# Low parts of sixteen query-weight tiles and four expert tiles split in the feed-forward on VectorE and kept in DRAM, and compressed inputs split in halves

## The chip, the cores and the metric

The kernel runs on one core of a Trainium2 chip. The metric is the device time of one execution in microseconds. TensorE (PE in the profile) does the matmuls; VectorE (DVE), ScalarE (ACT) and GpSimd (POOL) do the element-wise work; SyncE (SP) issues the loads of weights. fp32 products are made of three matmuls of a reduced type (fp32r): each operand is split into a high part and the low part that is left over.

## The reference, cut to what matters

Two blocks of a network on 512 tokens of width 1024. In the first the feed-forward matters here, in the second the compressed keys and values of the attention and the queries of a layer with 16384 experts (PEER).

```python
def hybrid_layer(x, p_i, ...):
    ...
    h = rmsnorm(x, g_ffn)
    g, u = jnp.split(h @ w_gate_up, 2, axis=-1)
    x = x + (jax.nn.silu(g) * u) @ w_down
    ...

def nsa_mixer(q, k_cmp, v_cmp, ...):
    ...
    def compress(t, w1, w2):
        blk = t[:, cmp_idx] + cmp_pos[:, None, :]
        blk = blk.transpose(0, 1, 3, 2, 4).reshape(B, n_cmp, G, CMP_LEN * dk)
        return jax.nn.gelu(blk @ w1) @ w2

    kc = compress(k_cmp, cmp_k_w1, cmp_k_w2)
    vc = compress(v_cmp, cmp_v_w1, cmp_v_w2)
    ...

def peer_ffn(x, w_q, sub_keys, expert_u, expert_v):
    q = _rms((xt @ w_q).reshape(T, P_HEADS, P_KEY_DIM)).astype(x.dtype)
    s1 = jnp.einsum('thd,hnd->thn', q[..., :half], sub_keys[:, 0])
    s2 = jnp.einsum('thd,hnd->thn', q[..., half:], sub_keys[:, 1])
    v1, i1 = lax.top_k(s1, P_TOPK)
    v2, i2 = lax.top_k(s2, P_TOPK)
    ...
    def chunk(args):
        xc, ec, gc = args
        a = jnp.einsum('cd,ckd->ck', xc, expert_u[ec])
        w = (gc * jax.nn.gelu(a)).astype(x.dtype)
        return jnp.einsum('ck,ckd->cd', w, expert_v[ec])
    ...
```

## The kernel before, in words

Activations lie transposed, 128 features by 512 tokens to a tile. A weight tile is 128x1024 fp32 (512 KB). `weights` (L50) brings one in: `load` (L45) issues a DMA on SP's queue into one of three `wraw` buffers, and `split` (L57) makes the high part `whi` by a cast on ACT (L58) and the low part `wlo` by a subtract (L59), on DVE, or on POOL where the caller says so. `whi` and `wlo` have two buffers each. `mm3` (L66) is one product: weights high by x high (L71), weights high by x low (L72), weights low by x high (L73). `linear` (L79) does a whole tile: 8 times `mm3`, 24 matmuls into one PSUM bank.

Each engine has a program in a fixed order, written by a scheduler; SP issues all loads of weights from one program, in order, and a DMA whose buffer is not free holds up those behind it.

The first block ends with `ffn` and `ple`. `ffn` goes over 44 w_gu tiles in pairs (gate and up); a pair's products on DVE are L229 and L231 to L233, and the low part `fl` of the result (L59 by way of `split`). Then come 8 rounds of three w_down pieces.

In the second block `compress` (L919) is called twice, for keys (kv=0) and values (kv=1). It splits its input `blk` into `bs` (L943; one buffer for both calls), on DVE for the keys and on POOL for the values, and multiplies by four weight tiles: for each of 16 positions a matmul with the high part (L949) and one with the low part (L950).

`queries` (L1414) takes the 8 heads of the PEER layer in turn. Each has two weight tiles (halves), the first's low part made on DVE, the second's on POOL:

```python
w = [s.weights(I["peer_w_q"][2 * h + half], D, G if half else V) for half in range(2)]
```

Between heads it makes the hidden values of expert chunks (`hidden`, `hidden_chunk`, L1655 and L1671; one weight tile `peer_ut` each), the first ones from a list AWAY whose results are stored to `spill`: none for heads 0 to 2, one for head 3, two for each later head, and 11 behind the last. On DVE stand, beside the low parts, the choice of the 16 best keys (`choose_steps`, L1563) and the norm of x (L1549), whose product xn is split into xsh (ACT) and xsl (DVE, L64).

Of the kernel before, what the change touches and what calls it, by code (L numbers as in the profile page):

```python
# [11 lines left out]
F32 = mybir.dt.float32  # L12
# [6 lines left out]
KF = 22  # L19
WARM = 9  # L20
# [5 lines left out]
class K:  # L26
    def __init__(s, tc, I, O, ctx):
        s.tc, s.nc, s.I, s.O = tc, tc.nc, I, O
        s.cst = ctx.enter_context(tc.tile_pool(name="cst", bufs=1))
        s.res = ctx.enter_context(tc.tile_pool(name="res", bufs=2))  # L30
        s.wp = ctx.enter_context(tc.tile_pool(name="wp", bufs=2))
        s.psum_stack = ctx.enter_context(ExitStack())
        s.n = 0
        s.banks(8)
# [15 lines left out]
    def weights(s, src, n, eng=None):  # L50
        raw = s.load(src, n)
        hi = s.wp.tile([128, 1024], F32R, tag="whi", name=s.name("whi"))
        lo = s.wp.tile([128, 1024], F32R, tag="wlo", name=s.name("wlo"))
        s.split(raw[:, :n], hi[:, :n], lo[:, :n], eng)
        return hi, lo

# [22 lines left out]
    def linear(s, src, a, nk=KD, eng=None, bank=()):  # L79
# [3 lines left out]
        for k in range(nk):  # L83
            s.mm3(ps, w, a, k, k, k == 0, k == nk - 1)
        return ps
# [59 lines left out]
    def block1(s):  # L145
# [50 lines left out]
        with ExitStack() as c1:  # L196
# [13 lines left out]
            x1 = s.ffn(act, xh, xl, sq, x1)  # L210
            x1 = s.ple(act, xh, xl, x1)
        return x1

    def ffn(s, act, xh, xl, sq, x):
# [3 lines left out]
        with tc.tile_pool(name="fa", bufs=1) as fa, tc.tile_pool(name="fk", bufs=2) as fk:  # L218
# [17 lines left out]
            for c in range(KD):  # L236
                ps = s.psum()
                for k0, k1 in ((0, 8), (8, 15), (15, 22)):
                    w = s.weights(I["w_down"][c][:, k0 * 128:k1 * 128], (k1 - k0) * 128)
                    for k in range(k0, k1):  # L240
                        s.mm3(ps, w, (fh, fl), k - k0, k, k == 0, k == KF - 1)
                TT(x1[:, c, :], ps, x[:, c, :], op=ALU.add)
# [260 lines left out]
class K2(K):  # L503
# [415 lines left out]
    def compress(s, ap, kv, ps, r):  # L919
# [22 lines left out]
        bs = ap.tile([128, 16, 2, 64], F32R, tag="bs", name=s.name("bs"))  # L942
        s.split(blk, bs[:, :, 0, :], bs[:, :, 1, :], s.nc.gpsimd if kv else None)  # L943
        ph = s.turns(*TB_)
        for q in range(4):
            wh, wl = (x.rearrange("p (a b) -> p a b", a=4) for x in s.weights(I[("cmp_k_w1", "cmp_v_w1")[kv]][q], 1024, CWE and s.nc.gpsimd))
            for i in range(4):
                j = q * 4 + i
                mm(ph[:, 0:256], bs[:, j].rearrange("p a b -> p (a b)"), wh[:, i, :], start=j == 0, stop=False, skip_group_check=True)  # L949
                mm(ph[:64, 0:256], bs[:, j, 0, :], wl[:, i, :], start=False, stop=j == 15, skip_group_check=True)  # L950
# [432 lines left out]
class K3(K2):  # L1383
    def experts(s, hT):
# [29 lines left out]
    def queries(s, ctx, eT):  # L1414
# [58 lines left out]
        for h in range(8):  # L1473
            qT = qk.tile([128, 2, T], F32, tag="qT", name=s.name("pqT"))
            ss = []
            w = [s.weights(I["peer_w_q"][2 * h + half], D, G if half else V) for half in range(2)]
# [194 lines left out]
    def hidden_chunk(s, c, eng):  # L1671
        w = s.weights(s.I["peer_ut"][c], D, eng)
        ps = s.pp.tile([128, 512], F32, tag="po", name=s.name("psA"), bufs=2)
        for k in range(KD):
            s.mm3(ps[:, :TD], w, (s.xh[:, :, 128:], s.xl[:, :, 128:]), k, k, k == 0, k == KD - 1)
# [190 lines left out]
LAG = 32  # L1866
# [52 lines left out]
```

## Time and profile before

| | before |
|---|---|
| median of 3 runs | 2421.92 us (2421.37 to 2426.93) |
| the profiled execution, its own time | 2424.03 us |
| its span in the profile | 2422.3 us |
| PE busy | 2365.4 us, 98% |
| DVE busy | 1779.3 us, 73% |
| ACT busy | 1018.3 us, 42% |
| POOL busy | 688.1 us, 28% |
| granted TensorE clock, mean over the span | 0.991 |
| read from and written to DRAM | 401.71 MB, 30.41 MB |

The span is the time from the first to the last instruction that the profiler saw. Busy time is a share of the whole span, so an engine may be idle in one stage and full in another. A wait in the profile is put down to the instruction that ended last of those waited for. A granted clock of 1 is 2.4 GHz.

### The profile page before, as it was taken

To read this page: it belongs to the slowest core of one execution; us is meant where nothing else is said; L and a number is where in the kernel's file an instruction comes from. 1 tells how busy PE (TensorE), PEld (TensorE's weight loads), DVE (VectorE), ACT (ScalarE), POOL (GpSimd) and SP (SyncE) were. 2 spreads that over 40 slices of the span, in tenths; PEclk is the share of its full clock that TensorE was granted. 3 is DMA by queue.
4 is the path that set the end of the run, shared out by engine and by line. 5 is a ranking of instruction groups with operands and counts; after the bars stand their busy time and mean duration, and the time that the engine had idled before them with its cause. 6 is when DMAs were issued, how large, how long until landed. Compare 5 with 4: busy or idle time off the path is not lost.

```text
span 2422.3 us, 34482 instructions
## 1 busy us (share of the span) xinstructions
PE 2365.4 (98%) x12831; PEld 2027.7 (84%) x12831; DVE 1779.3 (73%) x3426; ACT 1018.3 (42%) x1634; POOL 688.1 (28%) x693
## 2 busy tenths in 40 slices
PE   8999999999999999999799999999899999999999
PEld 7888888888888777677688999998798889989887
DVE  7777664555435658776899898796788878889797
ACT  5444343222224466763344555433333333333333
POOL 1000001000011204334455000255555555555441
PEclk9999999999999999999899999999999999999999
DMA  4232322222333331002133555648999999999895
GB/s 134 96 105 90 102 96 96 96 96 96 97 96 108 106 105 44 1 1 84 59 119 128 179 218 207 226 160 290 333 332 348 350 341 326 351 347 360 302 342 203
DMA packets 166072, 434.37 MB, mean 179 GB/s; under 512 B 15120, under 2 KB 71312, under 8 KB 164368
## 3 DMA queue, kind: packets, MB, share of 16 engines
q1 hardware_dynamic: 126736, 294.80, 36.1%
q0 software_dynamic: 36864, 134.23, 14.8%
q10 hardware_dynamic: 2304, 3.15, 0.3%
q8 instruction: 100, 1.64, 0.3%
q14 instruction: 68, 0.56, 0.1%
HBM read 401.71 MB, written 30.41 MB: 178 GB/s over the span
## 4 chain that ended last, share of the span: by engine, by line
PE 44%; DVE 5%; DMA 2%; ACT 1%; issue 1%; POOL 0%; ACTq 0%; DVEq 0%; POOLq 0%
PE ps L1792 7%; PE ps L1793 7%; PE psA L73 7%; PE psA L71 7%; PE ps L1791 7%; PE psA L72 6%; PE ps L1733 3%; DMA wraw<-peer_ut 1%; DVE wlo L59 1%; DMA wraw<-peer_v 1%; PE ps L73 0%; PE ps L71 0%; DVE ix L1583 0%; PE ps L72 0%; DVE ix L1580 0%
## 5 line engine op out<-in xcount | busy, mean ns | idle before, releaser
L58 ACT CAST whi<-wraw 128x1024 fp32r<-128x1024 f32 (+3 forms) x322 | 330.3, 1026 | 708.9 <-issue 250.1
L59 DVE TENSOR_TENSOR wlo<-wraw,whi 128x1024 fp32r<-128x1024 f32 (+2 forms) x314 | 387.6, 1235 | 205.4 <-ACT whi L58 197.3
L71 PE MATMUL psA<-xsh,whi 128*128 128x384 f32 x1024 | 346.6, 339 | 3.6 <-ACT whi L58 3.3
L73 PE MATMUL psA<-xsh,wlo 128*128 128x384 f32 x1024 | 345.3, 337 | 4.0 <-DVE wlo L59 4.0
L72 PE MATMUL psA<-xsl,whi 128*128 128x384 f32 x1024 | 343.5, 335 | 0.0
L72 PE MATMUL ps<-xl,whi 128*128 128x512 f32 x864 | 337.3, 390 | 4.3 <-DVE xl L64 4.3
L73 PE MATMUL ps<-xh,wlo 128*128 128x512 f32 x864 | 337.8, 391 | 0.5 <-DVE wlo L59 0.5
L71 PE MATMUL ps<-xh,whi 128*128 128x512 f32 x864 | 336.8, 391 | 0.7 <-ACT whi L58 0.5
L1792 PE MATMUL ps<-vl,wh 128*128 128x512 f32 x768 | 299.9, 390 | 3.9 <-DVE vl L59 3.9
L1793 PE MATMUL ps<-vh,wl 128*128 128x512 f32 x768 | 298.1, 389 | 0.0
L1791 PE MATMUL ps<-vh,wh 128*128 128x512 f32 x768 | 243.8, 390 | 4.5 <-ACT vh L58 4.5
L304 POOL TENSOR_TENSOR sq<-sq,sqt 128x512 f32<-128x512 f32 x18 | 28.8, 1601 | 711.9 <-ACT sqt L303 708.3
L71 PEld LDWEIGHTS psA<-xsh,whi 128*128 128x128 f32 x1024 | 192.4, 188 | 10.6 <-ACT whi L58 4.5
L73 PEld LDWEIGHTS psA<-xsh,wlo 128*128 128x128 f32 x1024 | 192.2, 188 | 8.2 <-DVE wlo L59 5.6
L72 PEld LDWEIGHTS ps<-xl,whi 128*128 128x128 f32 x864 | 162.5, 188 | 39.5 <-DVE xl L64 5.5
L72 PEld LDWEIGHTS psA<-xsl,whi 128*128 128x128 f32 x1024 | 192.4, 188 | 2.9
L73 PEld LDWEIGHTS ps<-xh,wlo 128*128 128x128 f32 x864 | 162.4, 188 | 36.9 <-DVE wlo L59 3.2
L71 PEld LDWEIGHTS ps<-xh,whi 128*128 128x128 f32 x864 | 162.5, 188 | 35.2 <-ACT whi L58 1.0
L58 ACT CAST wh<-w 128x384 fp32r<-128x384 f32 x128 | 65.7, 513 | 255.0 <-issue 150.5
L1792 PEld LDWEIGHTS ps<-vl,wh 128*128 128x128 f32 x768 | 144.1, 188 | 32.2 <-DVE vl L59 5.2
L1791 PEld LDWEIGHTS ps<-vh,wh 128*128 128x128 f32 x768 | 143.7, 188 | 32.0 <-ACT vh L58 5.7
L1793 PEld LDWEIGHTS ps<-vh,wl 128*128 128x128 f32 x768 | 144.2, 188 | 28.3
(549 smaller groups left out, 4676.9 us busy)
## 6 DMA issues: line engine op xcount, KB each, us to landing
wraw<-peer_ut SPq DMA_DIRECT2D x128, 512.0 KB, 5.2
wraw<-peer_v SPq DMA_DIRECT2D x128, 512.0 KB, 6.2
wraw<-w_in SPq DMA_DIRECT2D x58, 512.0 KB, 3.3
gdram<-blk SPq DMA_DIRECT2D x12, 2048.0 KB, 7.2
wraw<-w_gu SPq DMA_DIRECT2D x44, 512.0 KB, 3.2
gt<-gdram SPq DMA_DIRECT2D x32, 704.0 KB, 8.1
wraw<-w_out SPq DMA_DIRECT2D x16, 512.0 KB, 3.3
wraw<-peer_w_q SPq DMA_DIRECT2D x16, 512.0 KB, 3.3
```

Of the source, the lines that this page charges most:

```text
L58: s.nc.scalar.copy(hi, raw)
L59: (eng or s.nc.vector).tensor_tensor(lo, raw, hi.bitcast(F32), op=ALU.subtract)
L71: mm(ps, wh, ah[:, ka, :], start=start, stop=False)
L72: mm(ps, wh, al[:, ka, :], start=False, stop=False)
L73: mm(ps, wl, ah[:, ka, :], start=False, stop=stop)
L304: nc.gpsimd.tensor_tensor(sq[:, 0, :], sq[:, 0, :], t, op=ALU.add)
L1733: last = mm(ps[:, i * 128:i * 128 + 128], os[:, j * 4 + i], f[:, j * 4 + i], start=f is f0, stop=f is f2)
L1791: mm(Y[tt][b], wh[:, sl], vh[:, vs], start=False, stop=False, skip_group_check=True)
L1792: mm(Y[tt][b], wh[:, sl], vl[:, vs], start=False, stop=False, skip_group_check=True)
L1793: mm(Y[tt][b], wl[:, sl], vh[:, vs], start=False, stop=last, skip_group_check=True)
```

## The change

A generator, `ahead`, makes the low parts of 20 weight tiles early: the 16 tiles of peer_w_q and the first four chunks of AWAY. Each tile is taken in four quarters of 128x256. For each of the 80 pieces SP loads 128 KB into one of three buffers `alo`, DVE casts it to the one buffer `ahi`, DVE subtracts that from `alo` in place, and SP stores the result in a DRAM tile `lows`. `linear` and the w_down loop of `ffn` call `tick`, which emits pieces; in the scheduler's order they stand three to a w_gu tile, from the fifth tile on, and none in w_down. Later `weights` takes such a tile's low part by a DMA of 512 KB from `lows` into `wlo`; the high part is still a cast on ACT. For the four U chunks the matmuls stand in another order: all 16 with the high weights first, then the 8 with the low ones. In `compress` the block is cast and subtracted in two halves, each with two buffers, always on DVE.

```diff
+SHARE = 1.0
+EARLY = 20
+LOWS = 3
-    def weights(s, src, n, eng=None):
+    def weights(s, src, n, eng=None, low=None):
         raw = s.load(src, n)
         hi = s.wp.tile([128, 1024], F32R, tag="whi", name=s.name("whi"))
         lo = s.wp.tile([128, 1024], F32R, tag="wlo", name=s.name("wlo"))
-        s.split(raw[:, :n], hi[:, :n], lo[:, :n], eng)
+        if low is None:
+            s.split(raw[:, :n], hi[:, :n], lo[:, :n], eng)
+        else:
+            s.nc.scalar.copy(hi[:, :n], raw[:, :n])
+            s.nc.sync.dma_start(lo[:, :n].bitcast(F32), low)
         return hi, lo
...
+    def ahead(s, todo):
+        nc = s.nc
+        d = s.dram.tile([len(todo), 128, D], F32, name="lows")
+        pieces = [(i, slice(q * 256, q * 256 + 256)) for i in range(len(todo)) for q in range(4)]
+        made = []
+
+        def ask():
+            if len(made) < len(pieces):
+                i, sl = pieces[len(made)]
+                lo = s.home.tile([128, 256], F32R, tag="alo", name=s.name("alo"), bufs=LOWS)
+                nc.sync.dma_start(lo.bitcast(F32), todo[i][1][:, sl])
+                made.append(lo)
+
+        def store(n):
+            i, sl = pieces[n]
+            nc.sync.dma_start(d[i][:, sl], made[n].bitcast(F32))
+            if sl.stop == D:
+                s.low[todo[i][0]] = d[i]
+        ask()
+        for n in range(len(pieces)):
+            ask()
+            if n:
+                store(n - 1)
+            lo = made[n]
+            hi = s.home.tile([128, 256], F32R, tag="ahi", name=s.name("ahi"), bufs=1)
+            nc.vector.tensor_copy(hi, lo.bitcast(F32))
+            nc.vector.tensor_tensor(lo, lo.bitcast(F32), hi.bitcast(F32), op=ALU.subtract)
+            yield
+        store(len(pieces) - 1)
+        yield
...
+    def tick(s, share):
+        if s.early is not None:
+            s.due += share
+            while s.due >= 1:
+                s.due -= 1
+                next(s.early, None)
...
@@ -82,6 +133,7 @@
         ps = s.psum(*bank)
         for k in range(nk):
             s.mm3(ps, w, a, k, k, k == 0, k == nk - 1)
+        s.tick(SHARE)
...
-            x1 = s.ffn(act, xh, xl, sq, x1)
-            x1 = s.ple(act, xh, xl, x1)
+            with tc.tile_pool(name="early", bufs=1) as s.home:
+                s.early = s.ahead(s.later())
+                x1 = s.ffn(act, xh, xl, sq, x1)
+                x1 = s.ple(act, xh, xl, x1)
+                for _ in s.early:
+                    pass
+                s.early = None
...
@@ -239,6 +296,7 @@
                     w = s.weights(I["w_down"][c][:, k0 * 128:k1 * 128], (k1 - k0) * 128)
                     for k in range(k0, k1):
                         s.mm3(ps, w, (fh, fl), k - k0, k, k == 0, k == KF - 1)
+                    s.tick(SHARE * (k1 - k0) / 8)
...
-        bs = ap.tile([128, 16, 2, 64], F32R, tag="bs", name=s.name("bs"))
-        s.split(blk, bs[:, :, 0, :], bs[:, :, 1, :], s.nc.gpsimd if kv else None)
+        bs = [ap.tile([128, 8, 2, 64], F32R, tag="bs", name=s.name("bs"), bufs=2) for _ in range(2)]
+        for hf in range(2):
+            s.split(blk[:, hf * 8:hf * 8 + 8], bs[hf][:, :, 0, :], bs[hf][:, :, 1, :])
         ph = s.turns(*TB_)
         for q in range(4):
             wh, wl = (x.rearrange("p (a b) -> p a b", a=4) for x in s.weights(I[("cmp_k_w1", "cmp_v_w1")[kv]][q], 1024, CWE and s.nc.gpsimd))
             for i in range(4):
                 j = q * 4 + i
-                mm(ph[:, 0:256], bs[:, j].rearrange("p a b -> p (a b)"), wh[:, i, :], start=j == 0, stop=False, skip_group_check=True)
-                mm(ph[:64, 0:256], bs[:, j, 0, :], wl[:, i, :], start=False, stop=j == 15, skip_group_check=True)
+                mm(ph[:, 0:256], bs[j // 8][:, j % 8].rearrange("p a b -> p (a b)"), wh[:, i, :], start=j == 0, stop=False, skip_group_check=True)
+                mm(ph[:64, 0:256], bs[j // 8][:, j % 8, 0, :], wl[:, i, :], start=False, stop=j == 15, skip_group_check=True)
...
+    def later(s):
+
+        u = list(AWAY) + list(range(LAG))
+        todo = [(("q", i), s.I["peer_w_q"][i]) for i in range(16)] + [(("u", c), s.I["peer_ut"][c]) for c in u]
+        return todo[:EARLY]
...
-            w = [s.weights(I["peer_w_q"][2 * h + half], D, G if half else V) for half in range(2)]
+            w = [s.weights(I["peer_w_q"][2 * h + half], D, G if half else V, s.low.get(("q", 2 * h + half))) for half in range(2)]
...
     def hidden_chunk(s, c, eng):
-        w = s.weights(s.I["peer_ut"][c], D, eng)
+        low = s.low.get(("u", c))
+        w = s.weights(s.I["peer_ut"][c], D, eng, low)
         ps = s.pp.tile([128, 512], F32, tag="po", name=s.name("psA"), bufs=2)
-        for k in range(KD):
-            s.mm3(ps[:, :TD], w, (s.xh[:, :, 128:], s.xl[:, :, 128:]), k, k, k == 0, k == KD - 1)
+        x = s.xh[:, :, 128:], s.xl[:, :, 128:]
+        if low is None:
+            for k in range(KD):
+                s.mm3(ps[:, :TD], w, x, k, k, k == 0, k == KD - 1)
+        else:
+            for i, j in ((0, 0), (0, 1), (1, 0)):
+                for k in range(KD):
+                    s.nc.tensor.matmul(ps[:, :TD], w[i][:, k * 128:k * 128 + 128], x[j][:, k, :], start=i + j + k == 0, stop=i == 1 and k == KD - 1)
```

On SP in the feed-forward there were only the loads of w_gu, one to a tile (`wraw` are the load buffers). Before:

```order
L47 DMA wraw_428_2992<-w_gu 128x1024
L47 DMA wraw_432_3023<-w_gu 128x1024
L47 DMA wraw_438_3063<-w_gu 128x1024
L47 DMA wraw_442_3094<-w_gu 128x1024
L47 DMA wraw_448_3134<-w_gu 128x1024
```

In the changed kernel, `alo` being the buffers of the pieces and `lows` the DRAM tile (L80 loads a piece, L85 stores one, L54 loads a weight tile):

```order
L54 DMA wraw_481_3297<-w_gu 128x1024
L85 DMA lows_2938<-alo_513_3494 128x256
L85 DMA lows_2938<-alo_521_3540 128x256
L80 DMA alo_535_3623<-peer_w_q 128x256
L85 DMA lows_2938<-alo_527_3577 128x256
L80 DMA alo_541_3660<-peer_w_q 128x256
L80 DMA alo_549_3706<-peer_w_q 128x256
L54 DMA wraw_489_3343<-w_gu 128x1024
L85 DMA lows_2938<-alo_535_3623 128x256
L85 DMA lows_2938<-alo_541_3660 128x256
L85 DMA lows_2938<-alo_549_3706 128x256
L80 DMA alo_555_3743<-peer_w_q 128x256
```

Each w_gu load is now followed by three stores and three loads of pieces; a load of a piece stands behind the store that frees its buffer.

On DVE in the same place, one pair of w_gu tiles, before (`fg` is the product of gate and up, `fl` its low part):

```order
L229 TENSOR_TENSOR fg_436_3054<-ps_431_2998,r_425_2981 128x512
L59 TENSOR_TENSOR fl_2901<-fg_426_2983,fh_2900 128x512
L59 TENSOR_TENSOR wlo_440_3066<-wraw_438_3063,whi_439_3065 128x1024
L231 TENSOR_TENSOR fg_436_3054<-fg_436_3054,ft_437_3055 128x512
L232 TENSOR_TENSOR fg_436_3054<-fg_436_3054,r_425_2981 128x512
L233 TENSOR_TENSOR fg_436_3054<-ps_435_3029,fg_436_3054 128x512
L59 TENSOR_TENSOR wlo_444_3097<-wraw_442_3094,whi_443_3096 128x1024
L59 TENSOR_TENSOR fl_2901<-fg_436_3054,fh_2900 128x512
```

And in the changed kernel (L95 the cast of a piece, L96 its subtract; L286 and L288 to L290 are the products that were L229 and L231 to L233):

```order
L286 TENSOR_TENSOR fg_473_3251<-ps_464_3183,r_430_3000 128x512
L110 TENSOR_TENSOR wlo_477_3263<-wraw_475_3260,whi_476_3262 128x1024
L288 TENSOR_TENSOR fg_473_3251<-fg_473_3251,ft_474_3252 128x512
L95 CAST ahi_564_3792<-alo_555_3743 128x256
L289 TENSOR_TENSOR fg_473_3251<-fg_473_3251,r_430_3000 128x512
L96 TENSOR_TENSOR alo_555_3743<-alo_555_3743,ahi_564_3792 128x256
L95 CAST ahi_570_3829<-alo_563_3789 128x256
L96 TENSOR_TENSOR alo_563_3789<-alo_563_3789,ahi_570_3829 128x256
L95 CAST ahi_578_3875<-alo_569_3826 128x256
L96 TENSOR_TENSOR alo_569_3826<-alo_569_3826,ahi_578_3875 128x256
L290 TENSOR_TENSOR fg_473_3251<-ps_470_3220,fg_473_3251 128x512
L110 TENSOR_TENSOR wlo_483_3300<-wraw_481_3297,whi_482_3299 128x1024
```

The split of a weight tile (L110) now stands behind the casts and subtracts of three pieces.

On SP in the queries, heads 3 to 4, the loads of peer_w_q, keys and peer_ut stood alone. Before:

```order
L47 DMA wraw_1535_9883<-peer_ut 128x1024
L47 DMA wraw_1541_9918<-peer_w_q 128x1024
L47 DMA wraw_1544_9924<-peer_w_q 128x1024
L1429 DMA keys_1586_10214<-keys 128x256
L47 DMA wraw_1568_10107<-peer_ut 128x1024
L47 DMA wraw_1573_10141<-peer_ut 128x1024
L1429 DMA keys_1621_10459<-keys 128x256
L47 DMA wraw_1579_10176<-peer_w_q 128x1024
L47 DMA wraw_1582_10182<-peer_w_q 128x1024
```

In the changed kernel (L65 loads a low part, with the buffer `wlo` of the tile):

```order
L65 DMA wlo_1675_10203<-lows_2938 128x1024
L65 DMA wlo_1678_10209<-lows_2938 128x1024
L54 DMA wraw_1703_10411<-peer_w_q 128x1024
L54 DMA wraw_1706_10417<-peer_w_q 128x1024
L65 DMA wlo_1699_10379<-lows_2938 128x1024
L54 DMA wraw_1730_10600<-peer_ut 128x1024
L1495 DMA keys_1748_10707<-keys 128x256
L65 DMA wlo_1705_10414<-lows_2938 128x1024
L54 DMA wraw_1735_10634<-peer_ut 128x1024
L54 DMA wraw_1741_10669<-peer_w_q 128x1024
L65 DMA wlo_1708_10420<-lows_2938 128x1024
```

The low parts stand between the loads of whole tiles, each about two tiles behind its own `wraw` load.

## Rows read from the trace of the kernel before

**Rows 1.** The page: busy time of each engine, share of the span, instructions.
```profile
PE 2365.4 (98%) x12831; PEld 2027.7 (84%) x12831; DVE 1779.3 (73%) x3426; ACT 1018.3 (42%) x1634; POOL 688.1 (28%) x693
```

**Rows 2.** Windows view, feed-forward: length; PE, PEld, DVE, ACT, POOL busy; PEclk; DMA share; GB/s.
```profile
476.00:636.00 160.00, 160.00 (x707) 132.48 (x707) 83.11 (x102) 45.73 (x58) 0.00 (x0) 1.00 0.30 98
```

**Rows 3.** Timeline, PE, feed-forward: first matmuls of two w_gu tiles (start, length, us).
```profile
559.92 0.39 PE L71 MATMUL ps<-xh,whi 128*128 128x512 f32 x1
...
565.36 0.39 PE L71 MATMUL ps<-xh,whi 128*128 128x512 f32 x1
```

**Rows 4.** Timeline, DVE, the same stretch: one pair of w_gu tiles.
```profile
560.12 0.69 DVE L229 TENSOR_TENSOR fg<-ps,r 128x512 f32<-128x512 f32 x1 [2.71 <-PE ps L73]
561.02 1.22 DVE L59 TENSOR_TENSOR wlo<-wraw,whi 128x1024 fp32r<-128x1024 f32 x1 [0.21 <-ACT whi L58]
...
571.00 0.69 DVE L229 TENSOR_TENSOR fg<-ps,r 128x512 f32<-128x512 f32 x1 [2.71 <-PE ps L73]
```

**Rows 5.** One tile's instructions: lwl, 128x256 subtracts on DVE (ns, min/median/max).
```profile
L59 DVE TENSOR_TENSOR lwl<-wraw,lwh x8: 411/416/2022, 752.5 to 798.3; 128x256 fp32r<-128x256 f32 x8
```

**Rows 6.** One tile's loads: w_ple, 128 KB each, on SP's queue.
```profile
DMA to landing us min/median/max: 1.9/2.0/3.7
```

**Rows 7.** The stores to spill, 192 KB each, 1200 to 1345 us.
```profile
DMA to landing us min/median/max: 1.8/2.6/5.4
```

**Rows 8.** The three stores to spill of 1296 to 1312 us alone.
```profile
DMA to landing us min/median/max: 1.8/1.8/1.8
```

**Rows 9.** Waits of PE, 835 to 900 us (us in total, times, longest).
```profile
PE ps L949 <- POOL bs L59: 4.9, 1, 4.9
```

**Rows 10.** Timeline, POOL and PE, second compress.
```profile
854.48 2.34 POOL L59 TENSOR_TENSOR bs<-blk,bs 128x1024 fp32r<-128x1024 f32 x1 [9.85 <-ACT bs L58]
...
857.25 0.41 PE L950 MATMUL ps<-wlo,bs 128*64 128x256 f32 x1
...
857.46 0.41 PE L949 MATMUL ps<-whi,bs 128*128 128x256 f32 x1
...
863.52 0.28 PE L949 MATMUL ps<-whi,bs 128*128 128x256 f32 x1
...
863.63 0.28 PE L950 MATMUL ps<-wlo,bs 128*64 128x256 f32 x1
```

**Rows 11.** Waits of PE, 1140 to 1200 us.
```profile
PE ps L71 <- ACT xsh L63: 8.4, 2, 6.1
PE ps L73 <- DVE wlo L59: 4.3, 1, 4.3
PE ps L72 <- DVE xsl L64: 1.4, 1, 1.4
```

**Rows 12.** Waits of PE, 1200 to 1260 us.
```profile
PE psA L73 <- DVE wlo L59: 1.0, 2, 0.6
```

**Rows 13.** Waits of PE, 1260 to 1335 us.
```profile
PE psA L73 <- DVE wlo L59: 2.9, 2, 1.6
```

**Rows 14.** Timeline, DVE and POOL, PEER queries.
```profile
1159.78 0.60 DVE L64 SCALAR_TENSOR_TENSOR xsl<-xn,c_vec,xsh 128x384 fp32r<-128x384 f32 x1
...
1164.07 2.36 POOL L59 TENSOR_TENSOR wlo<-wraw,whi 128x1024 fp32r<-128x1024 f32 x1 [10.15 <-ACT whi L58]
...
1164.35 2.50 DVE L64 SCALAR_TENSOR_TENSOR xsl<-xn,c_vec,xsh 128x384 fp32r<-128x384 f32 x1
```

**Rows 15.** Timeline, PE, PEER queries, heads 2 and 3.
```profile
1186.35 0.39 PE L73 MATMUL ps<-xsh,wlo 128*128 128x512 f32 x1
...
1192.74 0.79 PE L73 MATMUL ps<-xsh,wlo 128*128 128x512 f32 x1 [4.31 <-DVE wlo L59]
1193.34 0.63 PE L71 MATMUL ps<-xsh,whi 128*128 128x512 f32 x1
1193.76 0.63 PE L72 MATMUL ps<-xsl,whi 128*128 128x512 f32 x1
```

**Rows 16.** DMA issues, 1140 to 1340 us (KB each, median us to landing).
```profile
wraw<-peer_w_q SPq DMA_DIRECT2D x12, 512.0 KB, 3.4
```

More of the change, by code (lines that the diff above doesn't have):

```diff
@@ L31, in __init__ @@
         s.wp = ctx.enter_context(tc.tile_pool(name="wp", bufs=2))
+        s.dram = ctx.enter_context(tc.tile_pool(name="dr", bufs=1, space=bass.MemoryType.DRAM))
         s.psum_stack = ctx.enter_context(ExitStack())
         s.n = 0
+        s.low = {}
+        s.early = None
+        s.due = 0.0
         s.banks(8)
@@ L209, in block1 @@
                     s.add_and_norm(I["w_out"], (mh, ml), xT, x1, "g_ffn", xh, xl, sq, wk)
-            x1 = s.ffn(act, xh, xl, sq, x1)
-            x1 = s.ple(act, xh, xl, x1)
+            with tc.tile_pool(name="early", bufs=1) as s.home:
[4 more added lines that the diff above has]
+                    pass
+                s.early = None
         return x1
```

## The prediction

> **What bounds the kernel now.** I read the page first: TensorE (PE) is busy 98% of the span, VectorE (DVE) 73%, GpSimd (POOL) 28% [rows 1]. So only the few idle stretches of PE, and those where its clock is low, can be won, and any new wait of PE is lost at once. The windows view shows the stretch into which the change puts work: in the feed-forward PE is busy for 160 of 160 us at a granted clock of 1.00 (of 2.4 GHz), DVE for 83 us, POOL for none [rows 2]. The timeline gives the pace there: the first matmuls of two w_gu tiles start 5.44 us apart [rows 3], and DVE's program repeats after two tiles, 10.88 us [rows 4]. The view of PE's waits shows what can be won: 4.9 us in the second `compress`, behind a subtract on POOL [rows 9], and in the PEER queries 4.3, 1.4, 1.0 and 2.9 us behind low parts of weights or of x [rows 11 to 13]. The 8.4 us for xsh in rows 11 come from the chain of the norm (columns, square root, rows, product), which the change leaves as it is.
>
> **A. The pieces in the feed-forward.** 80 pieces, each a load of 128 KB, a cast and a subtract of 128x256 on DVE, and a store of 128 KB. By the order there are three to a w_gu tile, so they fill some 27 tiles, 147 us.
>
> *DVE.* The subtract is 0.416 us [rows 5]. A DVE cast of this form is not in the trace; I bound it by 0.416 above (the same elements, one operand fewer) and by nothing below, and take 0.416, its nearest row. Three pieces to a tile are 6 x 0.83 = 5.0 us a pair, on top of 83.11/160 x 10.88 = 5.65 [rows 2]: 10.6 of 10.88 us. That fits, hidden under PE, with 0.2 us to spare. The Trainium skill ("VectorE: DVE Perf Modes", section "Mode 2×_2P — use both read ports for one tensor") lets a one-source copy in SBUF run at two elements a cycle, where a two-source subtract cannot: the cast would then be about 0.28 us (an estimate: from 0.416 for 256 elements and 1.22 for 1024, half the part that grows with them) and the pair 9.8 us. The cost is nothing by either; by the rule the margin is wider.
>
> *The buffers.* There are three `alo` buffers and SP issues in order: the load of piece n+3 stands behind the store of piece n and waits for its landing. One turn of a buffer is load 2.0 [rows 6], one product of the feed-forward that DVE may be in 0.69 [rows 4], cast 0.42, subtract 0.42, store 1.8, the three spill stores that had the queue to themselves, each larger than a piece [rows 8]: 5.3 us, against 5.44 for the tile that uses all three. What pieces delay is the split of the next w_gu tile: `wlo` is behind casts that wait for loads. Now it is done at 562.24 [rows 4], while the tile starts at 565.36 [rows 3] and needs it two matmuls later, at 565.8: 3.5 us of slack, once. So 26 turns of L us cost 26 x (L - 5.44) - 3.5: nothing up to L = 5.57. I take nothing (5.3 us). The upper end has the slowest w_ple load, 3.7 [rows 6]: L = 7.0, +37 us. The w_gu load ahead of each round on the same queue is what could make it so.
>
> **B. compress.** The second `compress` casts and subtracts its whole block only when the first has left the single `bs` buffer, and the subtract takes 2.34 us on POOL [rows 10], for which PE stands 4.9 us [rows 9]. Behind the gap 17 matmuls run at half clock, 1.2 GHz: 0.21 us apart where the later ones are 0.11 [rows 10], 1.6 us. With two half buffers the first half of the second block can be made while PE is in the second half of the first, and a half on DVE is 0.6 us (half of the 1.22 in rows 4). What is late next is the weights' own split: DVE needs 1.22 us for a tile that PE eats in 8 x 0.11 = 0.9; a first tile or two will wait for it. I take -4; ends 0 (the block itself is late) and -6.5 (gap and half clock both gone).
>
> **C. PEER queries.** Low parts arrive by DMA. Off go 8 subtracts on POOL, 8 on DVE, and 4 for U chunks.
> - xsl 0.60 us alone, 2.50 beside POOL's `wlo` subtract [rows 14]: -1.9, since PE waits for xsl, and the choice of keys and the norm stand behind it on DVE.
> - the gap of 4.3 us before head 3 [rows 11]: the low part lands 3.4 us [rows 16] after its buffer is free, at about 1186.4 with the last matmul of head 2 that reads it [rows 15], so at 1189.8 to 1190.8 (SP has other loads ahead), where PE stands for it from 1188.4 (1192.74 less the 4.3) [rows 15]: 1.4 to 2.4 us stay. -2.4.
> - 9 matmuls at half clock behind the gap, 0.42 apart [rows 15] where the pace is 0.227 [rows 3]: -1.8, since a gap half as long is nearer to those after which the clock stayed.
> - the 1.0 and half of the 2.9 us for `wlo` in rows 12 and 13 (the other half belongs to chunks that are split as before): -2.4.
> - what is late next: the low part of a first half waits for the two-buffer `wlo` ring behind a U chunk, two or three times 0.5 us: +1.2.
>
> Together -7.3. Ends: +3 (nothing gained, and such waits three times) and -12 (all of rows 12 and 13 and the 4.3 as well).
>
> **The sum.** 0 - 4 - 7.3 = -11.3, against the profiled execution of 2424.03 us, so 2413. That execution is 2.1 over the median of the three runs, 2421.92; against the median 2411. The 180 added DMAs (160 of 128 KB, 20 of 512 KB) all stand on SP's queue; their price is the one in A and C.
>
> **Rivals.**
> 1. *The piece loop is longer than a tile* (slower). Store, load, cast, subtract, store is one circle through SP's queue, and w_gu's load is in it. It decides from L = 5.57; the whole is slower than before by over 0.3% from L = 6.3 (26 x 0.86 - 3.5 = 19, less 11). If in two rounds of three a transfer meets the w_gu load and takes 3.7 instead of 2.0 [rows 6], L = 6.4: +22, 2433. For it: DMA runs beside PE at 0.30 of its engines' time already [rows 2], DVE has but 0.2 us to spare in a pair, and the slowest spill store took 5.4 [rows 7]. Against it: most of the small transfers are at 2.0 and below.
> 2. *Stores like the median one*, 2.6 us [rows 7]: L = 2.0 + 0.69 + 0.83 + 2.6 = 6.1, +14: 2425, no difference to be measured. The spill stores ran beside more traffic than the feed-forward has, which speaks against it. The Trainium skill ("DMA: Bandwidth & Descriptors", section "Anatomy of one DMA — SWDGE (gpsimd) path") puts a DMA at 2.0 us and its bytes at 436 GB/s, and says the confirmation is longest where the target is HBM, as these stores' is: 2.3 us each way (an estimate), the same L of 6.1. That is for another issuing path, and the 1.8 us of rows 8, for 192 KB to DRAM, are below it.
> 3. *The gains come back as other waits.* In the queries the chain for xsh (8.4 us) stays, and a wait removed ahead of it only makes it start to wait earlier; low loads go through one in-order queue with the wraw loads. Then only compress and xsl are left, -6, less 3 for late low loads: 2419, no difference.
>
> That the low parts are not used where they should be is excluded by the order: all 16 query tiles read them from DRAM.
>
> **How the numbers follow.** About 0.3%, 7 us, is what a measurement of this kernel can tell from no change: 2414.7 to 2429.2 is the same. Forecast 0.58 (its own range 2403 to 2415), rival 1 0.15, rival 2 0.12, rival 3 0.15. Faster 0.58, same 0.27, slower 0.15. The time is that of the forecast, 2411. The range reaches from the low ends of B and C, -6.5 and -12 (2421.9 - 18.5 = 2403), over rivals 2 and 3 to 2427, and leaves out rival 1 and a little at either end.
>
> **What would show it.** In the profile after: PE busy without a wait for `wlo` through the w_gu tiles, three pieces to each, DVE near 98% there; the lows stores landing in about 1.8 us. The row for POOL bs gone, and the second compress following the first within 2 us. xsl at 0.6 us throughout; the gap before head 3 at 1.4 to 2.4 us, now named for the DMA of `wlo`. It is wrong if w_gu tiles are over 5.5 us apart (rival 1 or 2, told apart by the stores' landing), or if the waits for xsh grow by what the others lose (rival 3).

## The result, and the profile after

The changed kernel is slower: 2449.25 us, the median of 4 runs (2443.81 to 2462.40), against 2423.26 us for the kernel before (4 runs). The ratio is 1.0106, with a 95% interval of 1.0081 to 1.0131. Its profiled execution took 2450.49 us with a span of 2448.3, 26.0 more than the span before. On the page, the busy line that answers to [rows 1]:

```profile
PE 2375.8 (97%) x12831; PEld 2028.2 (83%) x12831; DVE 1810.3 (74%) x3577; ACT 1019.6 (42%) x1636; POOL 660.8 (27%) x684
```

PE has 10 us more of busy time and still a smaller share, so it stands more. Where, is told by the start of the same matmuls in both traces:

| stretch, on PE | before | after | difference |
|---|---|---|---|
| start of the span to the first norm matmul behind w_gu (ps<-sq,ones) | 393.5 | 396.1 | +2.6 |
| from there to the first matmul of w_down (ps<-fh,whi) | 237.1 | 272.4 | **+35.3** |
| first to last matmul of both `compress` (ps<-whi,bs) | 22.5 | 19.2 | **-3.3** |
| first query matmul (ps<-xsh,whi) to the first transpose of `build` (ps<-ident,i) | 197.9 | 188.0 | **-9.9** |
| all the rest | | | +1.3 |

The second row of the table is called the loss in the feed-forward below, always against 237.1 us. The +2.6 lies in the first 25 us of the span. The rest is -1.5 in the matmuls between `ple` and `compress` and some +2.4 behind `build`. The first 25 us and the stretch behind `build` differ by as much between the profiles of all kernels below (the latter by up to 9 us), whatever was changed in them, and I leave them open.

**The feed-forward.** The windows view of the stretch of the pieces, answering to [rows 2]:

```profile
395.00:580.00 185.00, 159.73 (x683) 123.83 (x681) 123.71 (x251) 45.82 (x57) 0.00 (x0) 0.99 0.60 187
```

PE was busy 160 of 185 us, where it had been busy all the time; the DMA engines' share went from 0.30 to 0.60. The view of PE's waits for the whole feed-forward had no row before and has one now:

```profile
PE ps L124 <- DVE wlo L110: 27.1, 21, 2.4
```

The waits are 27.1 of the 35.3 us; the rest are matmuls that start further apart behind the gaps (462.07 and 462.41 behind one of them, 0.34 us where the pace is 0.227) and the short stretch of half clock named at the end.

The view of one tile's instructions, `alo`, has the casts and subtracts of the pieces on DVE and their loads and stores on SP (ns, min/median/max, then first and last start):

```profile
L95 DVE CAST ahi<-alo x80: 233/294/297, 393.7 to 579.3; 128x256 fp32r<-128x256 f32 x80
L96 DVE TENSOR_TENSOR alo<-alo,ahi x80: 415/425/427, 394.6 to 579.6; 128x256 fp32r<-128x256 f32 x80
...
L80 SPq DMA_DIRECT2D alo<-peer_w_q x64: 327/333/432, 391.4 to 539.2; - x64
L80 SPq DMA_DIRECT2D alo<-peer_ut x16: 328/333/437, 539.8 to 575.8; - x16
...
DMA to landing us min/median/max: 1.7/2.5/4.7
```

The 80 loads go from 391.4 to 575.8: 184.4 us for 79 steps, 7.00 us for three. That is the turn that the prediction put at 5.3 us. A landing took 2.5 us in the median of loads and stores together (I had taken 2.0 and 1.8), and the w_gu loads among them 4.2 where they had taken 3.2. DVE and SP show who stands for whom (waits in the same stretch, 400 to 590 us):

```profile
DVE ahi L95 <- DMA alo<-peer_w_q: 45.0, 36, 3.2
DVE ahi L95 <- DMA alo<-peer_ut: 12.3, 11, 2.3
```

```profile
SPq L80 <- DMA lows<-alo: 55.0, 41, 3.8
SPq L85 <- DVE ahi L95: 34.7, 28, 2.3
SPq L85 <- DVE alo L96: 22.3, 27, 2.1
```

DVE stands 57 us for loads of pieces, SP 55 us for stores to land before it may issue the next load, and 57 us for the casts and subtracts of what it is to store. Each is in order, so each round closes: load, cast, subtract, store, load. On DVE one round reads:

```profile
482.74 1.22 DVE L110 TENSOR_TENSOR wlo<-wraw,whi 128x1024 fp32r<-128x1024 f32 x1
483.87 0.69 DVE L288 TENSOR_TENSOR fg<-fg,ft 128x512 f32<-128x512 f32 x1
485.90 0.29 DVE L95 CAST ahi<-alo 128x256 fp32r<-128x256 f32 x1 [1.34 <-DMA alo<-peer_w_q]
486.11 0.68 DVE L289 TENSOR_TENSOR fg<-fg,r 128x512 f32<-128x512 f32 x1
486.71 0.42 DVE L96 TENSOR_TENSOR alo<-alo,ahi 128x256 fp32r<-128x256 f32 x1
487.17 0.29 DVE L95 CAST ahi<-alo 128x256 fp32r<-128x256 f32 x1
487.50 0.42 DVE L96 TENSOR_TENSOR alo<-alo,ahi 128x256 fp32r<-128x256 f32 x1
488.46 0.29 DVE L95 CAST ahi<-alo 128x256 fp32r<-128x256 f32 x1 [0.54 <-DMA alo<-peer_w_q]
488.78 0.43 DVE L96 TENSOR_TENSOR alo<-alo,ahi 128x256 fp32r<-128x256 f32 x1
489.13 0.68 DVE L290 TENSOR_TENSOR fg<-ps,fg 128x512 f32<-128x512 f32 x1
489.73 1.22 DVE L110 TENSOR_TENSOR wlo<-wraw,whi 128x1024 fp32r<-128x1024 f32 x1
```

The split `wlo` of the next tile comes 6.99 us after the last one (482.74 to 489.73), behind a cast that stood for its load. Its `whi` had been ready since 484.42, 5.31 us earlier. Before, DVE stood idle 0.21 us for `whi` and began `wlo` as soon as that was there [rows 4].

On SP the same stretch reads:

```profile
483.63 1.50 SPq L80 DMA_DIRECT2D alo<-peer_w_q  x3
485.22 0.38 SPq L54 DMA_DIRECT2D wraw<-w_gu  x1
487.16 1.11 SPq L85 DMA_DIRECT2D lows<-alo  x2
490.00 0.33 SPq L80 DMA_DIRECT2D alo<-peer_w_q  x1
```

The first of the loads at 483.63 is cast at 485.90, its subtract ends at 487.13, its store is issued at 487.16, and its buffer is loaded again at 490.00, when the store has landed. Over the 74 turns from the fourth piece on, the mean turn is 7.15 us: 2.7 until the load has landed, 0.3 until its cast, 0.95 to the end of its subtract, 0.35 until its store is issued, 2.7 until that has landed, 0.15 until the next load. So hardly anything in the turn is slack, and the two landings are 5.4 us of it.

**compress and the queries.** The waits of PE in compress and in the queries, answering to [rows 9] and [rows 11 to 13]:

```profile
PE ps L1010 <- DVE wlo L110: 3.7, 4, 1.2
```

```profile
PE ps L123 <- DVE xsl L115: 2.3, 2, 1.5
PE ps L124 <- DMA wlo<-lows: 2.0, 3, 1.1
PE psA L124 <- DVE wlo L110: 2.9, 2, 1.9
PE ps L122 <- ACT xsh L114: 1.8, 1, 1.8
```

```profile
1216.82 0.50 PE L124 MATMUL ps<-xsh,wlo 128*128 128x512 f32 x1 [1.07 <-DMA wlo<-lows]
```

POOL's 4.9 us are gone, and the weights' own split is what is late now, as said. In the queries the 4.3 us before head 3 are down to 1.07, now for the DMA of `wlo`; two further such waits, in heads 5 and 6, make it 2.0 us together. The waits of the U chunks (psA) for `wlo` went from 3.9 us [rows 12, 13] to 2.9. The waits for xsh, 8.4 us, are down to 1.8. In pieces_only and bs_only below, where no query reads the early low parts, they are 8.4 as before, so it is the making of low parts in the queries that had held the chain on DVE that feeds xsh, which I had not seen. How much of that is the longer xsl and how much the subtracts themselves is not shown. xsl is at 0.60 us throughout (longest 0.63, before 2.50).

### The profile page after: what moved, and what is told of

The parts are those of the page before. It is cut to its first block, busy times and chain, and to the rows that moved or that the text cites. A ratio compares the mean times of both kernels' runs of the same rounds, so it can differ in the third digit from the quotient of the medians.

```text
span 2448.3 us, 35013 instructions
## 1 busy us (share of the span) xinstructions
PE 2375.8 (97%) x12831; PEld 2028.2 (83%) x12831; DVE 1810.3 (74%) x3577; ACT 1019.6 (42%) x1636; POOL 660.8 (27%) x684
## 4 chain that ended last, share of the span: by engine, by line
PE 76%; DMA 10%; DVE 9%; ACT 2%; issue 2%; SPq 0%; POOL 0%; DVEq 0%; ACTq 0%; POOLq 0%
PE ps L124 10%; PE ps L123 10%; PE ps L122 10%; PE ps L1866 6%; PE psA L124 6%; PE ps L1867 6%; PE psA L122 6%; PE ps L1865 6%; PE psA L123 6%; DMA lows<-alo 3%; PE ps L1807 3%; DMA wraw<-peer_ut 3%; DMA alo<-peer_w_q 2%; PE ps L635 2%; DVE wlo L110 1%
## 5 line engine op out<-in xcount | busy, mean ns | idle before, releaser
L109 ACT CAST whi<-wraw 128x1024 fp32r<-128x1024 f32 (+2 forms) x302 | 309.1, 1024 | 555.2 <-PE ps L123 211.7
L110 DVE TENSOR_TENSOR wlo<-wraw,whi 128x1024 fp32r<-128x1024 f32 (+2 forms) x302 | 373.0, 1236 | 177.5 <-ACT whi L109 171.0
L122 PE MATMUL psA<-xsh,whi 128*128 128x384 f32 x992 | 336.6, 339 | 2.1 <-ACT whi L109 1.8
L124 PE MATMUL psA<-xsh,wlo 128*128 128x384 f32 x992 | 334.8, 338 | 3.7 <-DVE wlo L110 3.7
L123 PE MATMUL psA<-xsl,whi 128*128 128x384 f32 x992 | 333.4, 336 | 0.0
L1865 PE MATMUL ps<-vh,wh 128*128 128x512 f32 x768 | 251.7, 392 | 4.8 <-ACT vh L109 4.8
L122 PEld LDWEIGHTS psA<-xsh,whi 128*128 128x128 f32 x992 | 186.8, 188 | 9.3 <-ACT whi L109 3.3
L124 PEld LDWEIGHTS psA<-xsh,wlo 128*128 128x128 f32 x992 | 186.8, 188 | 7.9 <-DVE wlo L110 5.2
L123 PEld LDWEIGHTS psA<-xsl,whi 128*128 128x128 f32 x992 | 186.9, 188 | 2.7
L110 DVE TENSOR_TENSOR vl<-wraw,vh 128x1024 fp32r<-128x1024 f32 x128 | 156.2, 1221 | 23.0 <-ACT vh L109 21.2
```

The costliest lines, as they stand in the source:

```text
L109: s.nc.scalar.copy(hi, raw)
L110: (eng or s.nc.vector).tensor_tensor(lo, raw, hi.bitcast(F32), op=ALU.subtract)
L122: mm(ps, wh, ah[:, ka, :], start=start, stop=False)
L123: mm(ps, wh, al[:, ka, :], start=False, stop=False)
L124: mm(ps, wl, ah[:, ka, :], start=False, stop=stop)
L1865: mm(Y[tt][b], wh[:, sl], vh[:, vs], start=False, stop=False, skip_group_check=True)
```

## Experiments

The losses in the feed-forward, and the pieces to a w_gu tile in the scheduler's order:

| run | pieces a tile | ratio to before, 95% | loss, us |
|---|---|---|---|
| the change | 3 | 1.0106 (1.0081 to 1.0131) | 35.3 |
| pieces_only | 3 | 1.0157 (1.0136 to 1.0178) | 40.7 |
| bs_only | none | 0.9984 (0.9970 to 0.9999) | 0.0 |
| paced | 1 | 0.9961 (0.9941 to 0.9980) | 0.0 |
| paced13 | 1.3 | 0.9948 (0.9934 to 0.9962) | 0.0 |
| paced16 | 1 | 0.9986 (0.9975 to 0.9998) | 0.1 |
| paced20d | 1 | 0.9954 (0.9938 to 0.9970) | 0.0, and 4.3 in w_down |
| paced2 | 2 | 0.9985 (0.9972 to 0.9998) | 11.7 |
| two_rings | 2 | 1.0069 (1.0054 to 1.0084) | 32.5 |
| two4 | 2 | 1.0029 (1.0009 to 1.0048) | 17.9 |
| two4_late | 2 | 1.0081 (1.0054 to 1.0108) | 34.0 |
| four3 | 2.25 | 1.0062 (1.0046 to 1.0077) | 28.9 |
| four4 | 2.25 | 1.0079 (1.0049 to 1.0108) | 32.7 |
| small3 | 3, half as large | 1.0029 (1.0012 to 1.0045) | 5.2 |
| small6 | 3, half as large | 1.0004 (0.9986 to 1.0021) | 0.0 |
| no_dve | 3 to 4 | 1.0069 (1.0050 to 1.0088) | 32.1 |
| gu_act | 3 | 1.0105 (1.0083 to 1.0127) | 37.2 |
| no_dve_gu_act | 3 to 4 | 1.0064 (1.0038 to 1.0089) | 31.2 |
| wlo_pool | 3 | 1.0108 (1.0049 to 1.0168) | 38.6 |

**1. The parts alone.** pieces_only makes and stores the pieces and reads none of them; bs_only is the kernel before with the halves of compress.

```diff
-                s.low[todo[i][0]] = d[i]
+                pass
```

> The 80 pieces are made and stored as in the change, three to a w_gu tile, but nothing reads them: queries, U chunks and compress are as before. Theory 1 (three buffers turn once per w_gu tile and a turn takes 7.0 us where the tile takes 5.44): the whole loss stands here, about +35 us, 2458. Rival (the loss belongs to the change as a whole, for instance to the moved pools or to noise between executions): clearly under +35, below 2445.

> The kernel before with the halves of compress alone. Theory: 3 to 5 us faster, 2418 to 2420, the wait for POOL's subtract of 4.9 us gone. Rival: within 1 us of before, since the weights' own split sets the pace of the second compress.

pieces_only was slower than the change, by 38.5 us against before, with 40.7 in the feed-forward and no gain in the queries (199.0 us, before 197.9). bs_only took 3.3 us off the two compress, and its median is 4.0 below before (2422.21 against 2426.17). So the whole loss is that of the pieces, and the rest of the change gains 13 us.

**2. The pace.** In paced, DVE may take a piece only after the weight split of the tile at which the piece was asked for. That leaves one piece to a tile, over w_gu, w_down and ple.

```diff
+            with s.tc.issue_after(s.last_sub.ins):
-            nc.vector.tensor_copy(hi, lo.bitcast(F32))
-            nc.vector.tensor_tensor(lo, lo.bitcast(F32), hi.bitcast(F32), op=ALU.subtract)
+                nc.vector.tensor_copy(hi, lo.bitcast(F32))
+                nc.vector.tensor_tensor(lo, lo.bitcast(F32), hi.bitcast(F32), op=ALU.subtract)
```

paced2 sets SHARE to 2; paced13 has 1.3 pieces to a w_gu tile; paced16 sets EARLY to 16; paced20d has 1.75 to a full w_down tile.

> The change with each piece's cast and subtract put behind the weight split of its own tile on DVE, which leaves one piece to a tile, over w_gu, w_down and w_ple_gate. The same 80 pieces, loads and stores. Theory 1: a buffer has three tiles, 16 us, for a turn of 7, so no wait of PE in the feed-forward and the gains of compress and queries stay: 2408 to 2413. Rival theory 2 (each piece costs PE 0.44 us, by contention of its transfers or its time on DVE, however they are spread): as the change, 2444 to 2452.

> As the run before, two pieces to a w_gu tile. Theory 1: a buffer has one and a half tiles, 8.2 us, for a turn of about 7: no loss or a few us, 2408 to 2416. Theory 2: 2444 to 2452. Between the two (2425 to 2440) would speak for a turn that grows with the traffic itself.

> The run paced with the 16 query tiles alone, so that its pieces end with w_down. There paced had no wait of PE, and it lost 5.9 us in ple. Expected: nothing lost in the feed-forward or ple, the gains of compress and queries as in paced less a little for the four U chunks: 10 to 14 us below the kernel before. Rival (the loss in ple has another cause): as paced, 9 us below.

> The run paced with all 20 tiles, one piece to a w_gu tile and 1.75 to a w_down piece, so that they end with w_down. Expected, if pace is all: 11 to 15 us below the kernel before. Rival: where two pieces fall to a w_down tile the chain of store and load is again too long, and 3 to 8 us are lost there.

> The run paced with 1.3 pieces to a w_gu tile and one to a w_down tile, so that all 80 are done before ple: at most every third tile has two, which costs a chain of about 7 us once and is caught up in the next. Expected: no more than 2 us lost in the feed-forward and ple, the gains of compress (3 us) and queries (10 us) whole: 11 to 15 us below the kernel before. Rival: single tiles with two pieces already lose the 0.4 us each that paced2 lost, some 8 us together, and it comes out as paced, 9 below or less.

paced lost nothing to the end of w_down, with the same 80 pieces: a cost per piece, whatever the pace, is refuted. It lost 6 us in ple, where its last pieces fall. paced2 lost 11.7 (the expectation of two_rings below has 14.8 for it, by another reckoning); its 2423.46 us lie above theory 1's 2416 and just below the 2425 that would have spoken for a turn that grows with the traffic. paced13 differs from the change in pace and in this rule for DVE's order; paced2 and four3 have the same rule at two and 2.25 pieces a tile and still lose 11.7 and 28.9 us, so it is the pace that counts. paced13 lost nothing and keeps every gain, the fastest version of all: 2412.87 us, 0.9948 of before. The windows view of paced13, to be read beside the one above, and a stretch of its DVE:

```profile
395.00:580.00 185.00, 185.00 (x824) 152.51 (x824) 121.28 (x207) 57.28 (x72) 0.00 (x0) 1.00 0.50 157
```

```profile
484.82 0.69 DVE L290 TENSOR_TENSOR fg<-ps,r 128x512 f32<-128x512 f32 x1 [2.17 <-PE ps L128]
485.72 1.23 DVE L112 TENSOR_TENSOR wlo<-wraw,whi 128x1024 fp32r<-128x1024 f32 x1 [0.21 <-ACT whi L111]
486.86 0.29 DVE L97 CAST ahi<-alo 128x256 fp32r<-128x256 f32 x1
487.06 0.68 DVE L292 TENSOR_TENSOR fg<-fg,ft 128x512 f32<-128x512 f32 x1
487.66 0.42 DVE L98 TENSOR_TENSOR alo<-alo,ahi 128x256 fp32r<-128x256 f32 x1
488.00 0.68 DVE L293 TENSOR_TENSOR fg<-fg,r 128x512 f32<-128x512 f32 x1
490.25 0.69 DVE L294 TENSOR_TENSOR fg<-ps,fg 128x512 f32<-128x512 f32 x1 [1.57 <-PE ps L128]
491.16 1.23 DVE L112 TENSOR_TENSOR wlo<-wraw,whi 128x1024 fp32r<-128x1024 f32 x1 [0.21 <-ACT whi L111]
```

DVE is as busy as in the change (121 and 124 us of 185), but no cast waits for a load, and each `wlo` starts as soon as its `whi` is there. SP still stands for stores to land, 113.7 us between 400 and 630 us, and PE loses nothing by it:

```profile
SPq L81 <- DMA lows<-alo: 113.7, 44, 4.3
```

paced16 was told wrong: it lost nothing in the feed-forward, but its queries gained 2.9 us only. With the four U chunks split as before, PE waits for their low parts:

```profile
PE psA L127 <- DVE wlo L111: 10.0, 3, 6.1
```

So the gain of the queries needs the low parts of the U chunks too. paced20d lost nothing in w_gu and 4.3 us in w_down, where two pieces fall to a tile, as its rival said.

**3. By which way it reaches PE.** no_dve leaves the cast and the subtract out; gu_act issues the w_gu loads from ACT; no_dve_gu_act does both; wlo_pool has the low parts of w_gu made on POOL.

```diff
-                pg = s.linear(I["w_gu"][j], (xh, xl))
+                pg = s.linear(I["w_gu"][j], (xh, xl), q=nc.scalar)
```

> Three pieces to a tile as in the change, each loaded and stored again, but cast and subtract are left out, so the low parts of the query tiles and of four U chunks are not low parts. Theory 1, by way of DVE (the split of the next w_gu tile stands behind casts that wait for loads): with no cast on DVE no wait of PE in the feed-forward, under 3 us. Rival (by way of SP: the w_gu loads, or their transfers, come late behind the pieces' DMAs on the one queue): 15 to 35 us stay, and PE's waits are then named for whi or for the w_gu load.

> The change, with the loads of w_gu issued from ACT's queue in place of SP's: no w_gu load stands behind a piece's store or load any more. DVE's order is the change's, three pieces to a tile, and the transfers are the same. If the way through DVE is enough by itself (the next tile's split stands behind casts that wait for loads): 15 to 35 us stay lost in the feed-forward, PE's waits named for wlo. If the way through SP's queue was needed: under 8 us.

> The same with cast and subtract left out as in the run no_dve (the low parts of the query tiles and of four U chunks are not low parts). Neither way to PE is left, and the traffic of three loads and three stores a tile stays. Theory (waiting in order, on SP and on DVE, is the whole price): 0 to 3 us lost in the feed-forward, where no_dve lost 32. Rival (the traffic itself, at 0.60 of the DMA engines' time, makes the w_gu loads late): 10 us or more stay.

> The change, with the low part of the w_gu tiles subtracted on POOL, which is idle there, in place of DVE. Three pieces to a tile, the order on SP as in the change, the same transfers. The split that PE needs no longer stands behind casts that wait for loads. If the way through DVE carries the loss: under 12 us lost in the feed-forward, PE's waits no longer named for wlo on DVE. If the way through SP (w_gu loads behind pieces' DMAs) is as long: 25 to 35 us lost as before.

I had expected one way to be the needed one. Each is enough alone, though no_dve, with nothing on DVE to wait for, has up to four pieces to a tile. Without DVE's part, PE waits for `whi` and `wlo` of w_gu loads that came late, since SP stood for pieces (waits of PE and SP in no_dve):

```profile
PE ps L119 <- ACT whi L106: 11.0, 11, 1.9
PE ps L121 <- DVE wlo L107: 7.8, 15, 0.5
```

```profile
SPq L54 <- DVE wlo L107: 40.9, 9, 5.5
SPq L85 <- DMA alo<-peer_w_q: 34.6, 34, 2.4
SPq L80 <- DMA lows<-alo: 32.8, 26, 3.3
```

With the w_gu loads off SP, PE waits for `wlo` behind DVE's casts as in the change, 26.8 us, and no `whi` waits for its own load (one stands 4.8 us for a piece's store, by the third tie named below). With the w_gu tiles' `wlo` on POOL, the pieces on DVE delay the products fg, ACT waits for fg with ft and fh, `whi` stands behind those on ACT, and POOL's `wlo` behind `whi`:

```profile
PE ps L124 <- POOL wlo L110: 29.0, 22, 2.0
```

```profile
ACT fh L109 <- DVE fg L290: 75.6, 14, 7.0
ACT ft L287 <- DVE fg L286: 65.8, 14, 6.3
```

no_dve_gu_act does not tell what it was made for. A third tie showed: its program tells the landing of every DMA on one of eight semaphores (DMAHW0 to DMAHW7), shared by both queues, and a w_gu load on ACT can stand for a piece's store on SP. Such a load reads in its program, and in ACT's timeline:

```
L54 DMA wraw_479_3313<-w_gu 128x1024 [waits DMAHW7_49,DVE_49]
```

```profile
446.01 0.34 ACTq L54 DMA_DIRECT2D wraw<-w_gu  x1
446.39 1.04 ACT L106 CAST whi<-wraw 128x1024 fp32r<-128x1024 f32 x1 [14.64 <-DMA lows<-alo]
```

ACT idled 14.64 us there. Whether the traffic of three full pieces alone, without any tie, would cost PE something stays open.

**4. Buffers and order.** two_rings gives the loads two buffers and cast, subtract and store two others. small3 and small6 have pieces of 128x128 of 10 tiles, with three and six buffers. four3 and four4 have full pieces, cast in two halves, with three and four buffers. two4 is four4 with two pieces to a tile, and two4_late puts each load on SP behind the store two pieces later:

```diff
-                nc.sync.dma_start(lo.bitcast(F32), todo[i][1][:, sl])
+                with s.tc.issue_after(stores[len(made) - 2].ins) if len(made) >= LOWS else ExitStack():
+                    nc.sync.dma_start(lo.bitcast(F32), todo[i][1][:, sl])
```

> The change with the same 4 KB of buffers divided otherwise: two alo for the loads, two ahi that take cast, subtract and store. A load then waits for the subtract two pieces back and not for a store's landing. The scheduler puts two pieces to a w_gu tile, as in the run paced2, which lost 14.8 us in the feed-forward. Theory 1 (the turn load, cast, subtract, store, load is what is too long): 0 to 4 us lost there, since the chain is cut in two. Rival (the traffic of two pieces beside a w_gu load, and their time on DVE, set the loss): 12 to 18 us as in paced2.

> 80 pieces of 128x128 (10 query tiles only; the other six and the U chunks are split as before), three buffers, three pieces to a w_gu tile, the split of the tile ahead of its pieces on DVE. The control of the next run. Theory 1 (the turn of a buffer, load, cast, subtract, store, load, must fit the tiles that its ring spans: one tile here): still 15 to 35 us lost in the feed-forward, as half the bytes shorten a turn of 7 us little.

> The same pieces, DMAs, order on SP and work on DVE, with six buffers in place of three. Theory 1: a buffer has two tiles, 10.9 us, for its turn, so 0 to 3 us lost in the feed-forward. Rival (the number of DMAs on SP's queue, their traffic beside w_gu, or the pieces' place on DVE): the same loss as small3, within 5 us.

> All 80 pieces of 128 KB, each cast and subtracted in two halves of 128x128 (so that ahi is half as large), three alo buffers; the order has some 2.25 pieces to a w_gu tile. The control of the next run. Theory 1: three buffers span 1.33 tiles, 7.25 us, and a turn was 7.1 us in the change and 8.7 in paced2: 5 to 30 us lost in the feed-forward.

> The same with a fourth alo buffer in the room won, the same pieces, DMAs and work on DVE, nearly the same order. Theory 1: four buffers span 1.78 tiles, 9.7 us: 0 to 3 us lost. Rival (the traffic or number of full pieces): the loss of four3 within 4 us.

> As four4 (pieces of 128 KB, four buffers, cast and subtract in halves) with two pieces to a w_gu tile. On SP stands w_gu load, two stores, two loads, and each load waits for a store just issued. Theory 3 (SP's own round is the bound: it stands for the landing of stores that it has just issued, behind a w_gu load, whatever the buffers): 8 to 30 us lost in the feed-forward. The control of the next run.

> The same, with each load put on SP behind the store two pieces later, so that the store it waits for was issued most of a tile earlier: w_gu load, store, load, store, load. The same pieces, buffers, DMAs a tile and work on DVE. Theory 3: SP waits for no store's landing, and 0 to 5 us are lost. Rival (traffic and the number of full pieces a tile, or DVE's order): as two4, within 4 us.

small3 and small6 differ in buffers alone, and the loss goes with them, 5.2 and 0.0, so that the number of DMAs to a tile, three loads and three stores as in the change, costs nothing by itself at half the size; but small3 lost far less than I had expected: with half the bytes three pieces took 5.84 us (80 loads from 389.6 to 543.3), near the tile's 5.44. At full size the theory of the buffers' turn fell: the fourth buffer won nothing (28.9 and 32.7 us). SP still puts each load right behind the store that it waits for, so the queue itself stands:

```profile
SPq L80 <- DMA lows<-alo: 128.0, 45, 4.0
```

The theory made from that, that SP's standing for stores is the bound, fell with two4_late: no store is waited for on SP any more, and the loss is larger than in two4. Now SP holds the w_gu loads for DVE:

```profile
SPq L54 <- DVE alo L100: 112.3, 37, 4.2
SPq L87 <- DVE ahi L99: 49.0, 36, 2.2
```

The view names a piece's subtract; by the timeline it is the `wlo` just ahead of it (486.64 and 1.22 long, the load issued at 487.89), and that `wlo` had stood behind a cast whose own load was issued behind the previous w_gu load. two_rings, above both values of its expectation, closes in another way: its casts stand 93.1 us for stores to land before they may use their buffer. What these pairs do show: with the same pieces and the same traffic to a tile, order alone moves the loss from 17.9 to 34.0 us (two4, two4_late), so the traffic is not the whole price.

**What stands after all runs.** In the change the turn of a buffer is a closed circle: 7.15 us with 0.8 of standing in it, against 5.44 for the tile. At two or more full pieces to a tile, a round of SP and DVE, both in order, holds landings of 2.5 us and more (medians of load and store: 2.5 and 2.5 in the change, 2.6 and 3.4 in paced2, 2.5 and 4.5 in two4), the issues and DVE's work, and whichever link was cut another held PE up. At one piece a tile, a load has landed at least 5.8 us before its cast, at 1.3 at least 3.0 (4.8 in the median); no cast waits for its load, and what SP stands for is over in time. Shown are the pace (by paced13 against paced2 and four3), the turn of the change (by its trace), and that neither DVE's way, nor SP's, nor the number of full buffers alone is the cause. Why a landing takes 2.7 us in the mean there, and how much of the loss the traffic would keep without the ties, isn't settled.

## Why the prediction was wrong

It forecast 2411 us and was 38 off; rival 1, given 0.15, was the case that came, with 16 us more than its 2433.

- **A, the step that failed:** "One turn of a buffer is load 2.0 [rows 6], ... store 1.8 ...: 5.3 us", "I take nothing". The turn was 7.00 us, and the loss 35.3 where I had 0. The mechanism was named, and the formula fits: 26 x (7.0 - 5.44) - 3.5 = 37. What failed is the size of two terms: the load, 2.0, took 2.7 in the mean, and the store, 1.8, took 2.7, together 1.6 us of the 1.8 by which the mean turn is longer than 5.3. Each landing was read where few transfers were under way (w_ple, three spill stores). In the change seven DMAs share each round, and a landing is 2.5 us in the median. The standing between the links, 0.8 us, is near the 0.69 that I had allowed for a product on DVE. The medians beside traffic that I had in hand, 2.0 and 2.6 [rows 6, 7], already gave 6.1 us; that was rival 2, and I gave it 0.12.
- **The 3.5 us of slack:** a slack that is used once does not help against a round that is too long 26 times. A sum of 5.3 against 5.44 should have been told as a coin's toss.
- **DVE's time** was within what I had allowed: the cast took 0.294 us (I had taken 0.416) and the subtract 0.425. The Trainium skill's rule on a one-source copy ("VectorE: DVE Perf Modes", section "Mode 2×_2P — use both read ports for one tensor") had given 0.28, an estimate; the trace agrees. DVE was busy 124 of 185 us: not its load but its standing in order cost the time.
- **The Trainium skill on a DMA's price** ("DMA: Bandwidth & Descriptors", section "Anatomy of one DMA — SWDGE (gpsimd) path") had given 2.3 us each way by its fit, an estimate for another issuing path, and spoke against this change. The trace had 2.5 in the median and 1.7 at the shortest; I set the page aside for three rows of 1.8, and it was the nearer.
- **B**, -4: -3.3 measured, the wait gone and the weights' split late next, as said.
- **C**, -7.3: -9.9 measured, and that the two are near is in part luck. xsl came out at 0.60 as told, but PE's wait for it grew from 1.4 to 2.3. The gap before head 3 shrank to 1.07 us, below the 1.4 to 2.4 told; the two other waits for a DMA of `wlo`, 0.9 us, are the +1.2. The waits of the U chunks gave 1.0 where I had 2.4. That the wait for xsh would stay was wrong: it fell from 8.4 to 1.8 us, which is 6.6 of the 9.9.
- **Rival 3** did not come: the gains of B and C are there whole, and paced13 shows them with nothing to pay.

## What to carry to other kernels

Work put beside a busy engine can have waits in the order of an engine or queue that the busy one needs, and still be free, as long as its round fits the pace of the busy engine. So count the rounds, and compare the round's length, with landings as they are beside the new traffic, with that pace. Where the two are close, do less a round and ask for the data a round or two ahead; here the same 80 pieces cost 35 us at three a tile and nothing at 1.3. The scheduler's own order had put three to a tile; the pace had to be set by hand.

## What the runs showed of the hardware that I had not expected

A cast of a piece on DVE, 0.29 us alone, took up to 2.23 beside a subtract on POOL in wlo_pool (start, length), as xsl took 2.50 for 0.60 in [rows 14]:

```profile
490.47 2.23 DVE L95 CAST ahi<-alo 128x256 fp32r<-128x256 f32 x1
```

```profile
489.90 2.65 POOL L110 TENSOR_TENSOR wlo<-wraw,whi 128x1024 fp32r<-128x1024 f32 x1 [4.47 <-ACT whi L109]
```

The cast begins while POOL's subtract runs (489.90 to 492.55) and ends 0.15 us after it. Such pairs kept that run from being a clean cut of DVE's way.

The half clock of [rows 10] came back in the feed-forward of the change for one short stretch alone, behind a gap of 2.06 us (0.66 granted from 484 to 489 us, with matmuls 0.43 us apart, 1.2 GHz), although PE stood 21 times for up to 2.4 us; behind the other gaps the granted clock stayed at 1.00, 2.4 GHz.
